# One-hot rows of a top-k expert layer stored as pairs of tokens instead of fours

## The chip, the cores and the metric

One core of a Trainium2 chip runs the kernel. The metric is the device time of one execution in microseconds. The kernel before takes 2242.8 us (median of 3 runs, 2241.6 to 2243.34).

## The reference

The reference is a small two-block network on 256 tokens of width 1024 (the second block adds 16 meta tokens). Each block ends in a layer of 16384 experts, of which every token chooses 8 heads x 16. What the change touches is the last part of this layer:

```python
idx  = top-k expert numbers of each token, 8 heads x 16      # expert = 128 * i + j
gate = softmax of their scores
act  = gelu(h . u_tab[idx])
out  = sum over the 128 choices of gate * act * v_tab[idx]
```

The kernel does not gather rows of u_tab and v_tab. It multiplies the tokens by all 16384 rows, takes gelu of everything, multiplies by a dense table of gates that is zero where an expert was not chosen, and multiplies the result by all of v_tab.

## The kernel before, in words

One expert layer (`peer`, run once for each block) has these stages. The queries and scores are computed; VectorE picks the top 16 of 16 lists (`choose`). Then `peer_act` runs a loop over 128 tiles of u: each tile is 24 matmuls (8 depth slices x 3, because every float32 factor is split in a high and a low part, L177 to L179) that give 128 experts x 256 tokens in PSUM; ScalarE takes gelu into the table `cb` (`evac`, L1107 and L1109). After that comes a loop over 128 tiles of v (`products`, L730).

The dense table of gates is built four tokens at a time by the generator `groups`, one group for each tile of u once `choose` is done, so 64 groups in each block. For a token t with 128 choices (on the partitions) it needs the sum over the choices of gate * onehot(i) x onehot(j). Three rows of numbers per token are ready in `lists`: i, j and the low part of the gate, all float16; the high part is rounded from `gates`. One group does the following.

- `hot(t0, 0)` (VectorE, L1002) compares `iota4` with i: for 4 tokens a 128 x 128 x 4 float16 tile `oi`, where the four tokens lie side by side behind each index, so an index is 8 bytes behind the one before.
- `weigh` makes `w`: four ScalarE activations (L1008), one for each token, multiply `oi` of that token by its gate; one VectorE multiply (L1009) by the low parts of the gates; then `hot(t0, 1)` (L1002) makes `oj`.
- `product` (TensorE, L1023) does 4 x 2 matmuls, each with its weight load: weights `oj` of one token, moving operand `w` (high, then low part), 128 columns, into a PSUM bank of 4 tokens x 128.
- `use` (VectorE, L1015) multiplies the part of `cb` that gelu has already filled by the PSUM tile; the rest is copied by ScalarE (L1036) and multiplied later, in `evac` (L1112).

The order of work is the order in which Python issues it; each engine runs its own stream in that order. `product` is put in a list, `middle`, and is issued by `tile_mm` between the 12th and 13th matmul of the next tile of u. Behind the 24 matmuls of a tile, ScalarE runs L1036, four times L1008, L1107, L1109 and the rounding of a later weight tile (L67); VectorE runs L1112, L1009, L1002 (`oj`), the subtraction for a weight tile (L70), L1015, L1002 (`oi`). Tiles of u come on SyncE's queue, 512 KB each, four buffers deep; their high and low parts are three deep. `choose` also reads the constant: its lookups (L970) take every fourth element of `iota4`.

Of the kernel before, what the change touches and what calls it, by code (L numbers as in the profile page):

```python
# [10 lines left out]
F16 = mybir.dt.float16  # L11
U32 = mybir.dt.uint32
AF = mybir.ActivationFunctionType
ALU = mybir.AluOpType
# [104 lines left out]
class Build:  # L119
# [743 lines left out]
    def peer_act(self, b, cpool, ps, cb, pair):  # L863

        nc, spawn = self.nc, self.spawn
# [9 lines left out]
        lists, gates = lg[:, :2 * T].bitcast(F16).rearrange("p (a t) -> p a t", a=4)[:, :3], lg[:, 2 * T:]  # L875
        iota = cb[:, 95, 0:128]
        nc.sync.dma_start(iota, self.A["iota"])
        nc.sync.dma_start(keys, self.A["keys" + b])
        iota4 = cpool.tile([128, 128, 4], F16, name="iota4")
        nc.vector.tensor_copy(iota4, iota[:, :, None].to_broadcast([128, 128, 4]))  # L880
        seen, rows, have = [0], [0], [0]
        def choose():

# [2 lines left out]
            def take(shape, dt=F32):  # L886
                n = int(np.prod(shape[1:]))
                t = scr[:, off[0]:off[0] + n]
                off[0] += n
                assert off[0] <= 8192  # L890
                if dt != F32:
                    t = t.bitcast(dt)
                if len(shape) == 2:
                    return t
                names = " ".join("abcd"[:len(shape) - 1])
                return t.rearrange("p (%s) -> p %s" % (names, names), **dict(zip("abcd", shape[1:])))
# [51 lines left out]
            for tt in range(2):  # L948
                off[0] = base
                ts, ti, bs, bp = top[tt]  # L950
                g0 = take([128, 128])
                g = g0.rearrange("p (a b) -> p a b", a=8)
                sm = take([128, 8])
                nc.vector.tensor_tensor(g, bs, bs[:, :, 0:1].to_broadcast([128, 8, 16]), op=ALU.subtract)
                nc.scalar.activation(g, g, AF.Exp)
                tf = take([128, 8, 2, 16])
                nc.vector.tensor_copy(tf, ti)
                ab = take([128, 2, 8, 16], U32)
                nc.vector.tensor_scalar(ab[:, 0], bp, 4, None, op0=ALU.logical_shift_right)
                nc.vector.tensor_scalar(ab[:, 1], bp, 15, None, op0=ALU.bitwise_and)  # L960
                af = take([128, 2, 8, 16])
                nc.vector.tensor_copy(af, ab)
                yield 1.0
                ij = take([128, 2, 8, 16])
                oh = take([128, 4, 16, 16])
                sh = [128, 4, 16, 16]
                for q in range(2):
                    for h0 in (0, 4):
                        hs = slice(h0, h0 + 4)
                        nc.vector.tensor_tensor(oh, iota4[:, None, None, 0:16, 0].to_broadcast(sh),  # L970
                                                af[:, q, hs, :, None].to_broadcast(sh), op=ALU.is_equal)
                        yield 1.1
                        nc.vector.tensor_tensor(oh, oh, tf[:, hs, q, None, :].to_broadcast(sh), op=ALU.mult)
                        yield 1.1
                        nc.vector.reduce_sum(ij[:, q, hs, :], oh, axis=AX.X)
                        yield 1.1
                nc.vector.reduce_sum(sm, g, axis=AX.X)
                nc.vector.reciprocal(sm, sm)
                nc.vector.tensor_tensor(g, g, sm[:, :, None].to_broadcast([128, 8, 16]), op=ALU.mult)
                yield 0.5  # L980
                p = ps.tile([128, 3, 128], F32, name="pl", tag="o")
                for q, src in enumerate((ij[:, 0], ij[:, 1], g)):
                    middle.append(lambda q=q, src=src: nc.tensor.transpose(
                        p[:, q, :], src.rearrange("p a b -> p (a b)"), self.ident))
                yield None
                ts = slice(tt * 128, tt * 128 + 128)
                nc.scalar.copy(lists[:, 0:2, ts], p[:, 0:2, :])
                nc.scalar.activation(gates[:, ts], p[:, 2, :], AF.Copy, scale=SCALE)

                hi = take([128, 64]).bitcast(F16)  # L990
                nc.scalar.activation(hi, p[:, 2, :], AF.Copy, scale=SCALE)
                nc.vector.tensor_sub(lists[:, 2, ts], gates[:, ts], hi)
                yield 0.5
        def groups():

            TG = 4

            sh = [128, 128, TG]

            def hot(t0, q):  # L1000
                o = cpool.tile(sh, F16, name="o" + "ij"[q], bufs=1 + q)
                nc.vector.tensor_tensor(o, iota4, lists[:, q, None, t0:t0 + TG].to_broadcast(sh), op=ALU.is_equal)  # L1002
                return o

            def weigh(t0, oi):
                w = cpool.tile([128, 2, 128, TG], F16, name="w", bufs=2)
                for j in range(TG):
                    nc.scalar.activation(w[:, 0, :, j], oi[:, :, j], AF.Copy, scale=gates[:, t0 + j:t0 + j + 1])  # L1008
                nc.vector.tensor_tensor(w[:, 1], oi, lists[:, 2, None, t0:t0 + TG].to_broadcast(sh), op=ALU.mult)  # L1009
                return hot(t0, 1), w  # L1010

            def use(t0, p):
                n = rows[0]
                c, pk = cb[:, :, t0:t0 + TG], p.rearrange("p t i -> p i t")
                nc.vector.tensor_tensor(c[:, :n, :], c[:, :n, :], pk[:, :n, :], op=ALU.mult)  # L1015
                copies = [(c[:, n:, :], pk[:, n:, :])] if n < 128 else []
                have[0] = t0 + TG
                return copies

            def product(p, oj, w):  # L1020
                for j in range(TG):
                    for q in range(2):
                        nc.tensor.matmul(p[:, j, :], oj[:, :, j], w[:, q, :, j], start=q == 0, stop=q == 1)  # L1023

            oi = hot(0, 0)
            yield
            w = weigh(0, oi)
            yield
            oi = hot(TG, 0)
            copies = []  # L1030
            for t0 in range(0, T, TG):
                p = ps.tile([128, TG, 128], F32, name="pg", **G[t0 // TG % 4])
                middle.append(lambda: product(p, *w))
                yield
                for c in copies:
                    nc.scalar.copy(*c)  # L1036
                nw = weigh(t0 + TG, oi) if t0 + TG < T else None
                yield
                copies = use(t0, p)
                if t0 + 2 * TG < T:  # L1040
                    oi = hot(t0 + 2 * TG, 0)
                w = nw
            for c in copies:
                nc.scalar.copy(*c)
            done[0] = True

        bg, credit, gg = choose(), [0.0], groups()
        busy, done = [True], [False]

# [28 lines left out]
        def tile_mm(kind):  # L1078
            wh, wl = (w.rearrange("p (k n) -> p k n", k=KC) for w in self.stream.get(kind))
            p = ps.tile([128, T], F32, name="pu", tag="mm", bufs=3)  # L1080
            for k in range(KC):
                if k == 4:
                    while middle:
                        middle.pop(0)()
                self.mm3(p, [((wh[:, k, :], wl[:, k, :]), (hh[:, k, :], hl[:, k, :]))], k == 0, k == KC - 1)
            self.step()
            return p
# [27 lines left out]
        for i in range(128):  # L1115
            p = tile_mm("u" + b)
# [613 lines left out]
```

## Time and profile before

| what | value |
| --- | --- |
| median of 3 runs | 2242.8 us |
| the profiled execution itself | 2251.93 us |
| its span, first to last instruction | 2250.1 us |
| TensorE matmul busy | 2210.9 us, 98% |
| TensorE weight load busy | 2024.1 us, 90% |
| VectorE busy | 1586.4 us, 71% |
| ScalarE busy | 1312.5 us, 58% |
| granted TensorE clock, mean | 0.998 of full speed |
| transfers, mean over the span | 172 GB/s |

Matmuls are pipelined, so the time of a stage is read from the distance between the starts of matmuls and not from the length of one record. Idle time of an engine that is not the bottleneck costs nothing. The groups run in two stretches of the span, 476 to 718 us and 1646 to 1889 us.

### The profile page before, as it was taken

What the parts mean: (1) busy time and instruction counts of PE and PEld (TensorE: products, weight loads), DVE (VectorE), ACT (ScalarE), POOL (GpSimd) and SP (SyncE); (2) the same over time, 40 slices, a digit from 0 to 9 for tenths busy, and PEclk for the clock granted to TensorE, in tenths of its full rate; (3) what the DMA queues carried; (4) which work ended last, traced back from release to release, by engine and by line L of the source; (5) the groups of instructions that cost most, each with busy time, mean ns of one, the idle gap of its engine ahead of it and who ended that gap; (6) DMA issues with size and microseconds to landing.
All of it is one profiled execution on the core that took longest, in us unless ns stands there. A gap on an engine that the chain in (4) does not pass through costs nothing.

```text
span 2250.1 us, 39324 instructions
## 1 busy us (share of the span) xinstructions
PE 2210.9 (98%) x15318; PEld 2024.1 (90%) x15318; DVE 1586.4 (71%) x3063; ACT 1312.5 (58%) x2480; POOL 0.2 (0%) x4
## 2 busy tenths in 40 slices
PE   6999999999999999999999999999999999999999
PEld 3998999999999888888888889999999999888887
DVE  5877699887777555665676556699877777555555
ACT  6565554567777444444675456544577776544443
POOL 0000000000000000000000000000000000000000
PEclk9999999999999999999999999999999999999999
DMA  7475556654444666776443336556654445666664
GB/s 263 157 241 184 199 178 188 177 171 141 141 141 142 196 192 194 214 228 208 152 130 94 91 106 181 162 177 188 178 161 141 141 140 160 188 192 193 195 192 154
DMA packets 108155, 386.49 MB, mean 172 GB/s; under 512 B 12784, under 2 KB 14128, under 8 KB 107712
## 3 DMA queue, kind: packets, MB, share of 16 engines
q1 hardware_dynamic: 107968, 383.98, 56.5%
q8 instruction: 120, 1.97, 0.4%
q14 instruction: 67, 0.55, 0.1%
HBM read 382.88 MB, written 1.05 MB: 171 GB/s over the span
## 4 chain that ended last, share of the span: by engine, by line
PE 93%; DVE 3%; ACT 3%; issue 1%; DMA 1%; SPq 0%; ACTq 0%; DVEq 0%
PE acc L730 31%; PE pu L179 12%; PE pu L177 12%; PE pu L178 11%; PE pg L1023 5%; PE pz L177 5%; PE pz L179 4%; PE pz L178 4%; DVE wlo L70 1%; ACT whi L67 1%; PE pa L1426 1%; PE sp L1070 1%; PE po L565 1%; PE S L1371 0%; DMA raw<-w_mod_a 0%
## 5 line engine op out<-in xcount | busy, mean ns | idle before, releaser
L70 DVE TENSOR_TENSOR wlo<-raw,whi 128x1024 fp32r<-128x1024 f32 x690 | 840.9, 1220 | 441.1 <-ACT whi L67 435.7
L67 ACT CAST whi<-raw 128x1024 fp32r<-128x1024 f32 x690 | 722.7, 1048 | 405.4 <-PE acc L730 349.0
L177 PE MATMUL pu<-hh,whi 128*128 128x256 f32 x2272 | 650.7, 286 | 0.0
L179 PE MATMUL pu<-hh,wlo 128*128 128x256 f32 x2272 | 637.2, 280 | 0.3
L178 PE MATMUL pu<-hl,whi 128*128 128x256 f32 x2272 | 637.0, 280 | 0.0
L179 PEld LDWEIGHTS pu<-hh,wlo 128*128 128x128 f32 x2272 | 430.4, 189 | 1.1 <-DVE wlo L70 1.1
L178 PEld LDWEIGHTS pu<-hl,whi 128*128 128x128 f32 x2272 | 431.2, 190 | 0.0
L177 PEld LDWEIGHTS pu<-hh,whi 128*128 128x128 f32 x2272 | 429.6, 189 | 0.0
L730 PE MATMUL acc<-whi,ch 128*128 128x512 f32 x1024 | 317.3, 390 | 0.0
L730 PE MATMUL acc<-wlo,ch 128*128 128x512 f32 x1024 | 316.6, 389 | 0.0
L730 PE MATMUL acc<-whi,cl 128*128 128x512 f32 x1024 | 316.5, 389 | 0.0
L730 PEld LDWEIGHTS acc<-whi,cl 128*128 128x128 f32 x1024 | 192.2, 188 | 40.0
L730 PEld LDWEIGHTS acc<-wlo,ch 128*128 128x128 f32 x1024 | 192.2, 188 | 39.9
L730 PEld LDWEIGHTS acc<-whi,ch 128*128 128x128 f32 x1024 | 191.6, 188 | 39.2
L1008 ACT ACTIVATE w<-oi,lists 128x128 f16<-128x128 f16 x512 | 192.8, 581 | 1.9 <-DVE oi L1002 1.4
L1109 ACT ACTIVATE cb<-pu 128x256 f32<-128x256 f32 (+32 forms) x250 | 82.2, 329 | 167.2 <-PE pu L179 166.9
L1015 DVE TENSOR_TENSOR cb<-cb,pg 128x248 f32<-128x248 f32 (+42 forms) x128 | 69.7, 544 | 114.9 <-ACT cb L1109 114.7
L1023 PE MATMUL pg<-w,oj 128*128 128x128 f16 x1024 | 142.2, 296 | 0.0
L1023 PEld LDWEIGHTS <-oj 128*128 128x128 f16 x1024 | 103.8, 118 | 6.8
L1107 ACT ACTIVATE gl<-pu 128x4 f32<-128x4 f32 (+21 forms) x132 | 37.3, 283 | 111.3 <-ACT w L1008 97.6
L706 DVE TENSOR_TENSOR cl<-cb,ch 128x256 fp32r<-128x256 f32 x256 | 96.4, 418 | 5.2 <-ACT ch L704 5.2
L177 PE MATMUL pz<-nh,whi 128*128 128x256 f32 (+1 forms) x328 | 97.0, 296 | 0.0
(420 smaller groups left out, 2928.7 us busy)
## 6 DMA issues: line engine op xcount, KB each, us to landing
raw<-u SPq DMA_DIRECT2D x256, 512.0 KB, 3.6
raw<-v SPq DMA_DIRECT2D x256, 512.0 KB, 3.7
raw<-w_mod_b SPq DMA_DIRECT2D x32, 512.0 KB, 4.3
raw<-pw_q SPq DMA_DIRECT2D x32, 512.0 KB, 3.8
raw<-w_in_z SPq DMA_DIRECT2D x28, 512.0 KB, 4.2
raw<-w_mod_a SPq DMA_DIRECT2D x16, 512.0 KB, 4.8
raw<-w_mix_out SPq DMA_DIRECT2D x8, 512.0 KB, 4.0
raw<-w_gv SPq DMA_DIRECT2D x8, 512.0 KB, 3.5
```

Of the source, the lines that this page charges most:

```text
L67: nc.scalar.copy(hi[:, :f], t[:, :f])
L70: nc.vector.tensor_sub(lo[:, :f], t[:, :f], hi[:, :f].bitcast(F32)), self.load_to(k + self.raw_bufs))
L177: self.nc.tensor.matmul(out, sh, mh, start=first and i == 0, stop=False)
L178: self.nc.tensor.matmul(out, sh, ml, start=False, stop=False)
L179: self.nc.tensor.matmul(out, sl, mh, start=False, stop=last and i == n - 1)
L706: nc.vector.tensor_sub(l[r], c[:, r, :], h[:, r, :].bitcast(F32))
L730: nc.tensor.matmul(acc[tt][dh], st[:, ts], mv[:, dh * 512:dh * 512 + 512], start=i == n == 0, stop=i == 127 and n == 2, skip_group_check=True)
L1008: nc.scalar.activation(w[:, 0, :, j], oi[:, :, j], AF.Copy, scale=gates[:, t0 + j:t0 + j + 1])
L1015: nc.vector.tensor_tensor(c[:, :n, :], c[:, :n, :], pk[:, :n, :], op=ALU.mult)
L1023: nc.tensor.matmul(p[:, j, :], oj[:, :, j], w[:, q, :, j], start=q == 0, stop=q == 1)
L1107: nc.scalar.activation(t[:, :n], p[:, :n], AF.Gelu)
L1109: nc.scalar.activation(row[:, n:], p[:, n:], AF.Gelu)
```

## The change

The four tokens of a group are stored as two pairs. A tile is now [pair 2][index 128][token of the pair 2] instead of [index 128][token 4], so an index of one token lies 4 bytes behind the index before instead of 8. The constant `iota4` (each index four times) becomes `iota2` (twice). The comparisons and the multiply go over a four-dimensional view, in which the numbers of two tokens repeat for 128 indices; the matmuls and the ScalarE activations address token j as pair j // 2, half j % 2. Counts of instructions, their elements and the order of work stay the same.

```diff
-        iota4 = cpool.tile([128, 128, 4], F16, name="iota4")
-        nc.vector.tensor_copy(iota4, iota[:, :, None].to_broadcast([128, 128, 4]))
+        iota2 = cpool.tile([128, 128, 2], F16, name="iota2")
+        nc.vector.tensor_copy(iota2, iota[:, :, None].to_broadcast([128, 128, 2]))
...
-                        nc.vector.tensor_tensor(oh, iota4[:, None, None, 0:16, 0].to_broadcast(sh),
+                        nc.vector.tensor_tensor(oh, iota2[:, None, None, 0:16, 0].to_broadcast(sh),
...
-            sh = [128, 128, TG]
+            sh = [128, TG // 2, 128, 2]
+
+            def of(q, t0):
+                l = lists[:, q, t0:t0 + TG].rearrange("p (g s) -> p g s", s=2)
+                return l[:, :, None, :].to_broadcast(sh)
...
-                nc.vector.tensor_tensor(o, iota4, lists[:, q, None, t0:t0 + TG].to_broadcast(sh), op=ALU.is_equal)
+                nc.vector.tensor_tensor(o, iota2[:, None].to_broadcast(sh), of(q, t0), op=ALU.is_equal)
...
-                w = cpool.tile([128, 2, 128, TG], F16, name="w", bufs=2)
+                w = cpool.tile([128, 2] + sh[1:], F16, name="w", bufs=2)
                 for j in range(TG):
-                    nc.scalar.activation(w[:, 0, :, j], oi[:, :, j], AF.Copy, scale=gates[:, t0 + j:t0 + j + 1])
-                nc.vector.tensor_tensor(w[:, 1], oi, lists[:, 2, None, t0:t0 + TG].to_broadcast(sh), op=ALU.mult)
+                    nc.scalar.activation(w[:, 0, j // 2, :, j % 2], oi[:, j // 2, :, j % 2], AF.Copy,
+                                         scale=gates[:, t0 + j:t0 + j + 1])
+                nc.vector.tensor_tensor(w[:, 1], oi, of(2, t0), op=ALU.mult)
...
-                        nc.tensor.matmul(p[:, j, :], oj[:, :, j], w[:, q, :, j], start=q == 0, stop=q == 1)
+                        nc.tensor.matmul(p[:, j, :], oj[:, j // 2, :, j % 2], w[:, q, j // 2, :, j % 2], start=q == 0,
+                                         stop=q == 1)
```

## Rows read from the trace of the kernel before

**Rows 1.** The page's busy times and its chain by line
```profile
PE 2210.9 (98%) x15318; PEld 2024.1 (90%) x15318; DVE 1586.4 (71%) x3063; ACT 1312.5 (58%) x2480; POOL 0.2 (0%) x4
...
PE acc L730 31%; PE pu L179 12%; PE pu L177 12%; PE pu L178 11%; PE pg L1023 5%; PE pz L177 5%; PE pz L179 4%; PE pz L178 4%; DVE wlo L70 1%; ACT whi L67 1%; PE pa L1426 1%; PE sp L1070 1%; PE po L565 1%; PE S L1371 0%; DMA raw<-w_mod_a 0%
```
**Rows 2.** Busy time by stretch: span; engines' busy us; granted clock; DMA share
```profile
476.00:718.00 242.00, 242.00 (x2052) 238.59 (x2052) 184.62 (x381) 189.90 (x512) 0.00 (x0) 1.00 0.48 140
...
1655.00:1890.00 235.00, 235.00 (x1992) 231.71 (x1990) 177.99 (x368) 183.47 (x494) 0.00 (x0) 1.00 0.47 141
```
**Rows 3.** The chain of waits in 476 to 718 us
```profile
by line: PE pg L1023 25.2%; PE pu L177 25.0%; PE pu L178 24.9%; PE pu L179 24.9%
...
495.78 0.95 PE pg L1023 x8
499.56 0.95 PE pg L1023 x8
```
**Rows 4.** TensorE around one product, in order of time: start, length, what
```profile
707.18 0.28 PE L179 MATMUL pu<-hh,wlo 128*128 128x256 f32 x1
707.31 1.11 PE L1023 MATMUL pg<-w,oj 128*128 128x128 f16 x8
...
708.37 0.28 PE L178 MATMUL pu<-hl,whi 128*128 128x256 f32 x1
...
709.78 0.28 PE L178 MATMUL pu<-hl,whi 128*128 128x256 f32 x1
```
**Rows 5.** Loop over v, matmuls of 512 columns in order of time
```profile
1000.41 0.62 PE L730 MATMUL acc<-whi,cl 128*128 128x512 f32 x2
1000.86 0.62 PE L730 MATMUL acc<-whi,ch 128*128 128x512 f32 x2
```
**Rows 6.** Matmuls and loads by line: busy us, mean ns, idle before
```profile
L1023 PE MATMUL pg<-w,oj 128*128 128x128 f16 x1024 | 142.2, 296 | 0.0
L1023 PEld LDWEIGHTS <-oj 128*128 128x128 f16 x1024 | 103.8, 118 | 6.8
```
**Rows 7.** Weight loads in order of time: f16, short float32; the latter by line
```profile
707.30 0.15 PEld L1023 LDWEIGHTS <-oj 128*128 128x128 f16 x2
...
29.13 0.56 PEld L375 LDWEIGHTS pmc<-ident,rows 4*128 4x128 f32 x8 [0.47 <-issue]
...
L375 PEld LDWEIGHTS pmc<-ident,rows 4*128 4x128 f32 x16 | 1.2, 136 | 2.5 <-ACT rows L369 2.0 <-issue 0.5
```
**Rows 8.** Plain float32 matmuls of 128 columns, in order of time
```profile
262.31 0.60 PE L1070 MATMUL sp<-cb 128*128 128x128 f32 x4
```
**Rows 9.** ScalarE through one group, in order of time, [idle before it]
```profile
703.86 1.49 ACT L1008 ACTIVATE w<-oi,lists 128x128 f16<-128x128 f16 x4
706.14 0.37 ACT L1107 ACTIVATE gl<-pu 128x240 f32<-128x240 f32 x1 [0.78 <-ACT w L1008]
```
**Rows 10.** ScalarE before the first group: two activations of 128 elements
```profile
474.42 0.28 ACT L988 ACTIVATE lists<-pl 128x128 f32<-128x128 f32 x1
...
474.58 0.28 ACT L991 ACTIVATE cb<-pl 128x128 f16<-128x128 f32 x1
```
**Rows 11.** Four instructions by line: lengths in ns, least/median/most
```profile
L1002 DVE TENSOR_TENSOR oj<-iota,lists x128: 412/418/423, 475.9 to 1882.4; 128x512 f16<-128x512 f16 x128
...
L1008 ACT ACTIVATE w<-oi,lists x512: 554/582/618, 475.6 to 1882.8; 128x128 f16<-128x128 f16 x171
...
L970 DVE TENSOR_TENSOR cb<-iota,cb x16: 1216/1218/1226, 410.1 to 1633.6; 128x1024 f32<-128x1024 f16 x16
...
L880 DVE CAST iota<-cb x2: 426/426/427, 257.4 to 1427.0; 128x512 f16<-128x512 f32 x2
```
**Rows 12.** Who waited for whom in 476 to 718: us, times, longest; one late product
```profile
DVE cb L1015 <- ACT cb L1109: 57.2, 63, 1.6
ACT gl L1107 <- ACT w L1008: 48.8, 61, 0.9
...
L1015 DVE TENSOR_TENSOR cb<-cb,pg 128x488 f32<-128x488 f32 x1 | 0.7, 665 | 0.7 <-ACT cb L1109 0.7
```

## The prediction

> **What bounds the kernel now.** I read the busy times and the chain first. TensorE is busy 98% of the span, and the chain that ended last lies almost wholly on it; the products of the gates (L1023) hold 5% of it [rows 1]. Next I asked for the two stretches in which groups are built: TensorE is busy 242.0 of 242.0 us and 235.0 of 235.0, at full granted clock, while VectorE and ScalarE are each busy about three quarters of the time [rows 2]. So what TensorE saves there is saved for good, until another engine becomes as long. The chain in the first stretch gives L1023 a quarter of the time, 0.95 us for each run of eight matmuls, and a group comes every 3.78 us (495.78 to 499.56) [rows 3].
>
> Then I went to one product in order of time. From the last matmul of the first half tile (707.18) to the second matmul of the second half (708.37) pass 1.19 us; twelve ordinary steps take 1.41 (708.37 to 709.78), 0.118 each. Taking off two such steps, the eight pairs of load and matmul cost 0.954 us, which agrees with the 0.95 of the chain: 0.119 us for each pair [rows 3, 4].
>
> This is odd, and the change rests on it. A matmul of 128 float16 columns costs as much as one of 256 split-float32 columns. What does a column cost? In the loop over v two matmuls of 512 columns take 0.452 us (1000.41 to 1000.86), 0.226 each [rows 5]. From 256 to 512 columns the step grows from 0.118 to 0.226, so 256 columns cost 0.109, 128 cost 0.0545, and about 0.009 is fixed for each pair [rows 4, 5]. At that rate 128 columns should take 0.0635. The pair takes 0.118: its columns come at half the rate. The record of one matmul says the same: 296 ns, longer than the 280 of 256 columns [rows 4, 6].
>
> Is the load what takes long instead? Its record has 118 ns, the same as the pair's distance, which is suspicious [rows 6]. But the first two loads of a run together end 0.15 us after the first began, and each lasts about 0.12, so the second began within some 0.03 of the first: a load can be taken in quickly [rows 7]. And eight short loads at L375 take 0.56 us together with 0.136 for each, so they start 0.06 apart, though each record is twice as long as that: a record's length is latency and not what a pair must wait [rows 7]. So I put the 0.118 down to the moving operand, whose columns lie 8 bytes apart in `w`, where the split-float32 ones lie 4 bytes apart and come at full rate.
>
> **The change part by part.** *The matmuls (L1023).* Number and columns stay; the step of both operands falls from 8 to 4 bytes, which is the step of the float32 operands that run at one column per step of the fast rate. I take the full rate: 0.118 becomes 0.0635, so 8 x 0.0545 = 0.436 us per group. Nothing else is on the path (TensorE has no idle time there), and there are 2 x 64 groups: 128 x 0.436 = 55.8 us. Bounds: without the fixed 0.009 a group would save 0.51 us, 65 us in all; if the columns keep their rate, nothing. A loss I leave out here: no row has a 4-byte step slower than this pair. Plain float32 at L1070 has a 4-byte step and comes every 0.11 us ((0.60 - 0.28) / 3) for 128 columns, also the half rate, but that is another kind of number [rows 8]; it counts for the third rival.
>
> [...]
>
> *Other waits in the group.* The period falls from 3.78 to 3.34 us. ScalarE idles 0.78 us per group before L1107 (waiting for the tile, though the row names its own last instruction), so 0.34 is left [rows 9, 12]. VectorE idles before L1015 57.2 / 63 = 0.91 us on average and about 0.7 late in the stage, when L1015 is longest; 0.26 is left there [rows 12]. Tiles of u come at 140 GB/s [rows 2], which becomes about 158, less than the 172 of the whole span. Nothing becomes late, but little is left.
>
> *VectorE's comparisons and multiply (L1002 twice, L1009).* Elements stay at 512. Now a run of two numbers repeats instead of four. I cost it at zero: L970 reads a number repeated in every element and still takes one element per step (1024 in 1218 ns), so a repeated word is no obstacle [rows 11]. Bounds: zero, or the rate of float32 products, 665 ns for 488 elements (so about 690 for 512) against 418, +0.27 each and +0.8 us per group [rows 11, 12]. I take zero, since the innermost run is still dense and even; above 0.26 per group it begins to show.
>
> *ScalarE's four activations (L1008).* They read and write every second number instead of every fourth. Four take 1.49 us with records of 0.58: one starts every 0.30 [rows 9, 11]. Dense ones start 0.16 apart (474.42 to 474.58) [rows 10]. Bounds: 0.16 (worth nothing, as ScalarE is off the path) to 0.58, one wholly after the other. I take 0.30 or less; ScalarE's idle time covers it up to 0.39.
>
> *The constant.* L880 copies 256 instead of 512 elements, twice: less than 0.43 us each, behind TensorE's query matmuls; zero. L970 reads every second instead of every fourth number at one element per step; zero [rows 11].
>
> **The sum.** The profiled execution took 2251.9 us, 1.8 more than its span of 2250.1. Minus 55.8 it is 2196.1. The median of the runs is 0.9960 of that execution, so 2187.
>
> **The rivals.**
> 1. *Full rate, as above:* 2187, chance 0.59. Its own range, with 50 to 65 us saved, is 2178 to 2193.
> 2. *The load becomes the bound.* The first f16 load of a run starts 0.12 after the matmul ahead of it, where a float32 load starts beside it [rows 4, 7]; perhaps it does not overlap with columns. Then the pair stops between 0.0635 and 0.118. Halfway, 0.09, it saves 8 x 0.028 x 128 = 29 us: 2214. Chance 0.15.
>  [...]
> 3. *The rate does not depend on 8 or 4 bytes* (any step of float16 halves it, or the load's 118 ns is what each pair waits for). Then 2243, no change. For it: each matmul begins as its load's record ends. Against it: rows 7. Chance 0.13.
> 4. *VectorE falls to the float32 rate.* Its work per group is 3.78 - 0.91 = 2.87 and becomes 3.67, longer than 3.34. VectorE then sets the pace and 0.11 x 128 = 14 us are saved: 2229. Chance 0.06.
> 5. *Slower: ScalarE's activations run one after the other.* Tokens of a pair now write the two halves of the same words over a denser range. Place: L1008; its work per group is 3.78 - 0.78 = 3.00 us, and four full records of 0.58 (2.33 instead of 1.49) make 3.84. That is over the present period by 0.06: 128 x 0.06 = +8 us, 2251. It eats into the gain from a spacing of 0.39 on and turns it to a loss from 0.50 on. Against it: tokens 0 and 1 share words already, at 0.30. Chance 0.07.
>
> **How the numbers follow.** The likeliest case gives 2187. The range 2178 to 2232 holds cases 1, 2 and 4, about 0.80; cases 3 and 5 are left out. This kernel's measurement tells about 0.2% (4.5 us) from no change. Faster by more: 0.59 + 0.15 + 0.06 = 0.80; within it 0.13; slower 0.07.
>
> **What would show it.** Right: L1023's matmul record falls from 296 to about 240 ns, its run of eight in the chain from 0.95 to about 0.52 us, a group comes every 3.34 us, TensorE stays without idle time in these stretches, L1002 and L1009 stay at 418 ns, and the idle time before L1107 falls to about 0.34 and before L1015 to about 0.5 on average. Wrong: a product that still takes 0.95 (case 3) or about 0.75 (case 2); 690 ns at L1002 with idle TensorE (case 4); L1008 starting 0.5 us apart (case 5). A gain of the other stages would mean that I missed something: all of it should lie in the two stretches.

## The result, and the profile after

The kernel after takes 2193.98 us (median of 4 runs, 2188.84 to 2196.8), against 2242.74 for the kernel before in the same comparison: a ratio of 0.9771, with a 95% interval of 0.9757 to 0.9785. A second comparison gave 2190.38 against 2245.29, 0.9757 [0.9743, 0.9771]. So 49 to 55 us went. The forecast was 2187, with 2178 to 2232 as its range. The profiled execution of the kernel after took 2196.02 us with a span of 2194.0, 56.1 less than the span before.

The busy times and the chain by line come first, as in [rows 1]:

```profile
PE 2156.2 (98%) x15318; PEld 1970.3 (90%) x15318; DVE 1585.6 (72%) x3063; ACT 1289.5 (59%) x2480; POOL 0.2 (0%) x4
...
PE acc L730 32%; PE pu L177 12%; PE pu L179 12%; PE pu L178 12%; PE pz L177 5%; PE pz L179 4%; PE pz L178 4%; PE pg L1029 3%; DVE wlo L70 1%; ACT whi L67 1%; PE pa L1433 1%; PE sp L1077 1%; PE po L565 1%; PE S L1378 1%; PE pu L224 1%
```

The numbers of instructions are the same as before on every engine, and TensorE is still busy 98%. It is busy for 55 us less (2210.9 before), and the share of the products on the chain falls from 5% to 3%. L1023 is L1029 now; L1002, L1009 and L1008 are L1007, L1015 and L1013; L1107, L1109 and L1015 are L1114, L1116 and L1021.

Then the two stretches in which groups are built, with the columns of [rows 2]:

```profile
476.00:690.00 214.00, 214.00 (x2045) 211.20 (x2043) 184.68 (x383) 178.78 (x510) 0.00 (x0) 1.00 0.53 157
...
1628.00:1835.00 207.00, 207.00 (x1973) 204.32 (x1973) 177.04 (x367) 170.42 (x488) 0.00 (x0) 1.00 0.54 158
```

These windows are chosen to hold nearly the same matmuls (2045 for 2052, 1973 for 1992), and they are 214 and 207 us long instead of 242 and 235. From the start of the first product to the start of the last pass 211.9 us in either block, where it was 238.8 and 239.0: 54.0 us less in all. TensorE still has no idle time in them, at full granted clock, and the DMA rate has risen from 140 to 157 GB/s. The chain in the first stretch, as in [rows 3]:

```profile
by line: PE pu L177 29.6%; PE pu L179 28.1%; PE pu L178 28.0%; PE pg L1029 14.3%
...
481.53 0.48 PE pg L1029 x8
488.25 0.48 PE pg L1029 x8
```

Between these two lies one more group: 6.72 us for two, 3.36 each, where a group took 3.78. One product in order of time (start, length, what), as in [rows 4]:

```profile
602.09 0.28 PE L179 MATMUL pu<-hh,wlo 128*128 128x256 f32 x1
602.22 0.64 PE L1029 MATMUL pg<-w,oj 128*128 128x128 f16 x8
602.66 0.36 PE L177 MATMUL pu<-hh,whi 128*128 128x256 f32 x1
602.86 0.28 PE L178 MATMUL pu<-hl,whi 128*128 128x256 f32 x1
```

From the last matmul before the run to the second one behind it pass 0.77 us. Less two ordinary steps of 0.118 that is 0.53 for the product, where the same sum gave 0.954 before [rows 4]. So a product saves 0.42, and 128 of them 54 us of the 56. The other 2 us lie outside the group stretches, where ordinary steps differ from one execution to the next (last section). Note that the step from L177 to L178 is 0.20 and not 0.118. It was so before, too, from this line to 708.37 [rows 4]:

```profile
708.17 0.36 PE L177 MATMUL pu<-hh,whi 128*128 128x256 f32 x1
```

So this step alone is no new cost, and only the sum up to L178 can be compared: from the start of the last float16 matmul to L178 pass 0.227 us now and 0.249 before (medians of the 128 products). Each pair became 0.06 shorter, this stretch only 0.022: the return to float32 costs something here that it did not cost before. The chain counts this at L177, which is why its share is larger than that of L178.

The matmul and the load of the product by line, as in [rows 6], and three instructions by line, as in [rows 11]:

```profile
L1029 PE MATMUL pg<-w,oj 128*128 128x128 f16 x1024 | 81.2, 220 | 0.0
L1029 PEld LDWEIGHTS <-oj 128*128 128x128 f16 x1024 | 58.9, 97 | 5.6
```

```profile
L1013 ACT ACTIVATE w<-oi,lists x512: 420/443/469, 476.8 to 1827.5; 128x128 f16<-128x128 f16 x171
...
L1007 DVE TENSOR_TENSOR oj<-iota,lists x128: 415/419/423, 477.2 to 1827.1; 128x512 f16<-128x512 f16 x128
...
L970 DVE TENSOR_TENSOR cb<-iota,cb x16: 1217/1218/1227, 410.9 to 1604.1; 128x1024 f32<-128x1024 f16 x16
```

The matmul's record fell from 296 to 220 ns, the load's from 118 to 97, ScalarE's activation from 582 to 443. VectorE's comparison stayed (418 before, 419 now), and so did L970. At last the waits, as in [rows 12] (total us, times, longest):

```profile
ACT gl L1114 <- ACT w L1013: 33.7, 61, 0.6
DVE cb L1021 <- ACT cb L1116: 30.2, 63, 1.2
```

ScalarE idles 33.7 / 61 = 0.55 us per group before L1114, VectorE 30.2 / 63 = 0.48 before L1021. Both have come nearer to setting the pace, and neither does.

### The profile page after: what moved, and what is told of

Its sections match the earlier page's. It is cut to its first block, busy times and chain, and to the rows that moved or that the text cites. A ratio compares the mean times of both kernels' runs of the same rounds, so it can differ in the third digit from the quotient of the medians.

```text
span 2194.0 us, 39324 instructions
## 1 busy us (share of the span) xinstructions
PE 2156.2 (98%) x15318; PEld 1970.3 (90%) x15318; DVE 1585.6 (72%) x3063; ACT 1289.5 (59%) x2480; POOL 0.2 (0%) x4
## 4 chain that ended last, share of the span: by engine, by line
PE 92%; DVE 3%; ACT 3%; DMA 1%; issue 1%; SPq 0%; ACTq 0%; DVEq 0%
PE acc L730 32%; PE pu L177 12%; PE pu L179 12%; PE pu L178 12%; PE pz L177 5%; PE pz L179 4%; PE pz L178 4%; PE pg L1029 3%; DVE wlo L70 1%; ACT whi L67 1%; PE pa L1433 1%; PE sp L1077 1%; PE po L565 1%; PE S L1378 1%; PE pu L224 1%
## 5 line engine op out<-in xcount | busy, mean ns | idle before, releaser
L177 PE MATMUL pu<-hh,whi 128*128 128x256 f32 x2272 | 649.3, 286 | 0.0
L178 PE MATMUL pu<-hl,whi 128*128 128x256 f32 x2272 | 635.6, 280 | 0.0
L178 PEld LDWEIGHTS pu<-hl,whi 128*128 128x128 f32 x2272 | 431.2, 190 | 0.0
L177 PEld LDWEIGHTS pu<-hh,whi 128*128 128x128 f32 x2272 | 426.7, 188 | 0.0
L1116 ACT ACTIVATE cb<-pu 128x256 f32<-128x256 f32 (+32 forms) x250 | 81.9, 328 | 163.6 <-PE pu L179 163.4
L1013 ACT ACTIVATE w<-oi,lists 128x128 f16<-128x128 f16 x512 | 170.3, 442 | 1.9 <-DVE oi L1007 1.4
L1021 DVE TENSOR_TENSOR cb<-cb,pg 128x248 f32<-128x248 f32 (+42 forms) x128 | 69.7, 544 | 60.7 <-ACT cb L1116 60.7
L177 PE MATMUL pz<-nh,whi 128*128 128x256 f32 (+1 forms) x328 | 97.0, 296 | 0.0
L179 PE MATMUL pz<-nh,wlo 128*128 128x256 f32 (+1 forms) x328 | 93.2, 284 | 0.0
L178 PE MATMUL pz<-nl,whi 128*128 128x256 f32 (+1 forms) x328 | 92.9, 283 | 0.0
L1114 ACT ACTIVATE gl<-pu 128x4 f32<-128x4 f32 (+21 forms) x132 | 37.3, 283 | 79.6 <-ACT w L1013 67.3
```

The source lines that it names most:

```text
L177: self.nc.tensor.matmul(out, sh, mh, start=first and i == 0, stop=False)
L178: self.nc.tensor.matmul(out, sh, ml, start=False, stop=False)
L179: self.nc.tensor.matmul(out, sl, mh, start=False, stop=last and i == n - 1)
L1013: nc.scalar.activation(w[:, 0, j // 2, :, j % 2], oi[:, j // 2, :, j % 2], AF.Copy, scale=gates[:, t0 + j:t0 + j + 1])
L1114: nc.scalar.activation(t[:, :n], p[:, :n], AF.Gelu)
L1116: nc.scalar.activation(row[:, n:], p[:, n:], AF.Gelu)
```

## The experiments

The theory after the result: a matmul's columns come at a rate set by the step of its moving operand `w`, and the weights' step hardly matters. The rivals: the load is what became faster (its record fell too, 118 to 97); or 8 bytes are as good as 4, as the forecast's third rival had it, and something else is at work. After that, the size: the run costs 0.53 where 8 x 0.0635 = 0.51 had been forecast. Is that the pair's own cost, or something that each run pays once?

**Only the moving operand at 4 bytes.** `oi` and `w` as in the kernel after; `oj`, the weights, in fours as before (`four` repeats the numbers of four tokens for 128 indices).

```diff
+        iota4 = cpool.tile([128, 128, 4], F16, name="iota4")
+        nc.vector.tensor_copy(iota4, iota[:, :, None].to_broadcast([128, 128, 4]))
...
+                if q == 1:
+                    o = cpool.tile([128, 128, TG], F16, name="o" + "ij"[q], bufs=1 + q)
+                    nc.vector.tensor_tensor(o, iota4, four(q, t0), op=ALU.is_equal)
+                    return o
...
-                        nc.tensor.matmul(p[:, j, :], oj[:, j // 2, :, j % 2], w[:, q, j // 2, :, j % 2], start=q == 0,
+                        nc.tensor.matmul(p[:, j, :], oj[:, :, j], w[:, q, j // 2, :, j % 2], start=q == 0,
```

> Only the moving operand w (and oi, from which it is made) is laid out in pairs, 4 bytes from one index to the next; the weights oj stay in fours, 8 bytes. Theory A (the step of the moving operand sets the rate of the columns): the matmul of L1023 is as in the changed kernel, record about 220 ns, pairs about 58 ns apart, a product about 0.53 us, a group every 3.36 us, time 2194 (2188 to 2200). Rival B (the weight load with its 8-byte step is what each pair waits for): as before, record 296, pairs 118 apart, a group every 3.78, time 2243. ScalarE's activations: about 440 ns under both, since w and oi have the new layout.

Measured: 2191.23 us, 0.9758 [0.9742, 0.9774]; the same as the kernel after. Its matmul and load (ns: least/median/most), and a product in order of time:

```profile
L1038 PEld LDWEIGHTS <-oj x1024: 111/113/136, 471.4 to 1828.0; 128*128 128x128 f16 x171
...
L1038 PE MATMUL pg<-w,oj x1024: 217/221/252, 471.4 to 1828.1; 128*128 128x128 f16 x171
```

```profile
602.14 0.28 PE L179 MATMUL pu<-hh,wlo 128*128 128x256 f32 x1
602.26 0.67 PE L1038 MATMUL pg<-w,oj 128*128 128x128 f16 x8
602.73 0.36 PE L177 MATMUL pu<-hh,whi 128*128 128x256 f32 x1
602.93 0.28 PE L178 MATMUL pu<-hl,whi 128*128 128x256 f32 x1
```

The product takes 0.79 - 0.236 = 0.55 us (0.558 as the median of all 128; the kernel after has 0.530). So the weights' step of 8 bytes costs 28 ns per product, and its record stays long (113) while the pairs follow each other in 59. All of the gain but these 28 of 424 ns is the moving operand's.

**Only the weights at 4 bytes.** The reverse: `oj` in pairs, `oi` and `w` in fours.

```diff
-                w = cpool.tile([128, 2] + sh[1:], F16, name="w", bufs=2)
+                w = cpool.tile([128, 2, 128, TG], F16, name="w", bufs=2)
...
-                        nc.tensor.matmul(p[:, j, :], oj[:, j // 2, :, j % 2], w[:, q, j // 2, :, j % 2], start=q == 0,
+                        nc.tensor.matmul(p[:, j, :], oj[:, j // 2, :, j % 2], w[:, q, :, j], start=q == 0,
```

> The other half alone: the weights oj in pairs (4 bytes), w and oi in fours (8 bytes). Theory A: no change of time, 2243 (2238 to 2248), pairs 118 ns apart, a group every 3.78 us, though the load's record may fall from 118 to about 97 ns. Rival B: all of the gain, 2194, pairs about 58 apart. If both halves are needed, this one and the moving half alone both stay at 2243.

Measured: 2241.77 us, 0.9991 [0.9977, 1.0004]: no change.

```profile
L1037 PEld LDWEIGHTS <-oj x1024: 96/116/119, 469.6 to 1874.0; 128*128 128x128 f16 x171
L1037 PE MATMUL pg<-w,oj x1024: 276/296/300, 469.6 to 1874.1; 128*128 128x128 f16 x171
```

The matmul's record is the old 296 ns, and a product costs 0.937 us as the median of all, 16 ns less than before. The load's record did not fall to 97 either but stayed at 116, while in the run just told it was 113 with pairs 59 apart: its length does not tell how long a pair takes. The load is not what the old pair waited for.

**The moving operand at 16 bytes.** `w` holds high and low part of four tokens side by side, so its columns lie 16 bytes apart; the weights stay in pairs.

```diff
-                w = cpool.tile([128, 2] + sh[1:], F16, name="w", bufs=2)
+                w = cpool.tile([128, 128, 2, TG], F16, name="w", bufs=2)
...
-                        nc.tensor.matmul(p[:, j, :], oj[:, j // 2, :, j % 2], w[:, q, j // 2, :, j % 2], start=q == 0,
+                        nc.tensor.matmul(p[:, j, :], oj[:, j // 2, :, j % 2], w[:, :, q, j], start=q == 0,
```

> High and low part of w are interleaved, so the moving operand's step becomes 16 bytes; weights in pairs (4 bytes), oi in fours. Theory A1 (a column costs one step of the fast rate for each 4 bytes of the operand's step): four steps a column, 213 ns for 128 columns, pairs 215 to 230 apart, record near 400 ns, a group every 4.6 to 4.7 us, time about 2243 + 1024 x 0.105 = 2350 (2335 to 2365). Rival A2 (any step above 4 bytes simply halves the rate): pairs 118 apart, 2243. [...]

Measured: 2354.08 us, 1.0489 [1.0471, 1.0506]. A product in order of time, the first stretch by engine, and ScalarE's activation:

```profile
600.35 0.28 PE L179 MATMUL pu<-hh,wlo 128*128 128x256 f32 x1
600.47 1.99 PE L1037 MATMUL pg<-w,oj 128*128 128x128 f16 x8
602.10 0.48 PE L177 MATMUL pu<-hh,whi 128*128 128x256 f32 x1
602.41 0.28 PE L178 MATMUL pu<-hl,whi 128*128 128x256 f32 x1
```

```profile
480.00:760.00 280.00, 280.00 (x1923) 230.07 (x1922) 177.44 (x362) 247.18 (x484) 0.00 (x0) 1.00 0.39 115
```

```profile
L1022 ACT ACTIVATE w<-oi,lists x512: 866/1096/1132, 468.6 to 1982.7; 128x128 f16<-128x128 f16 x171
```

The product takes 2.06 - 0.236 = 1.82 us (1.83 as the median): 0.229 for each pair. TensorE has no idle time, so this is its own pace and not a wait, although ScalarE's activation took 1096 ns. The rate went on falling in proportion to the step: 0.0575 at 4 bytes, 0.118 at 8, 0.229 at 16. A flat half rate for every float16 step that isn't dense is out with that. As an estimate from the loop over v [rows 4, 5], a column at the fast rate costs (0.226 - 0.118) / 256 us, or 0.42 ns; four of these for each of 128 columns make 0.216 us, where the expectation had 213 ns and the run shows 0.229.

**Dense.** Every one-hot row by itself, 2 bytes from one index to the next. That leaves one number of `lists` repeated 128 times in VectorE's innermost dimension.

```diff
-            sh = [128, TG // 2, 128, 2]
+            sh = [128, TG, 128]
...
-                l = lists[:, q, t0:t0 + TG].rearrange("p (g s) -> p g s", s=2)
-                return l[:, :, None, :].to_broadcast(sh)
+                return lists[:, q, t0:t0 + TG, None].to_broadcast(sh)
...
-                        nc.tensor.matmul(p[:, j, :], oj[:, j // 2, :, j % 2], w[:, q, j // 2, :, j % 2], start=q == 0,
+                        nc.tensor.matmul(p[:, j, :], oj[:, j], w[:, q, j], start=q == 0,
```

> All four tokens one behind the other, 2 bytes from one index to the next, for oi, oj and w. Theory A: the columns are at full rate already at 4 bytes, so pairs stay 57 to 58 ns apart and a product at 0.53 us. VectorE now repeats one number for 128 indices. If that costs its two-a-step rate (690 instead of 419 ns at each of three instructions, +0.8 us per group) VectorE sets the pace with 2.9 + 0.8 = 3.7 us per group, TensorE gets idle time, and the time is about 2194 + 128 x 0.33 = 2236 (2215 to 2245). If it does not, 2194 (2188 to 2200).

Measured: 2218.11 us, 0.9876 [0.986, 0.9893].

```profile
L1028 PE MATMUL pg<-w,oj x1024: 218/219/231, 477.5 to 1856.2; 128*128 128x128 f16 x171
...
L1006 DVE TENSOR_TENSOR oj<-iota,lists x128: 682/705/761, 476.8 to 1855.0; 128x512 f16<-128x512 f16 x128
```

```profile
480.00:700.00 220.00, 210.23 (x1970) 198.94 (x1968) 219.97 (x367) 173.07 (x492) 0.00 (x0) 1.00 0.50 149
```

```profile
PEld L1028 <- DVE oj L1006: 20.4, 55, 0.6
```

Two things are told apart here. The matmul gains almost nothing below 4 bytes: its record is 219 ns against 220, and pairs come every 0.056 (the median from start to start) instead of 0.0575. And VectorE's comparison takes 705 ns instead of 419, so VectorE is busy 219.97 of 220.00 us and TensorE waits for `oj`. This is the forecast's fourth rival, in a kernel that isn't the one forecast: what decides here is whether the innermost dimension holds two numbers (419 ns) or one (705). (The multiply, L1014 there, took 706.)

**Each product as two runs of four pairs.** The first two tokens behind the float32 matmuls of one step of the tile, the others behind a later step.

```diff
-            def product(p, oj, w):
-                for j in range(TG):
+            def product(p, oj, w, j0):
+                for j in range(j0, j0 + 2):
...
-                middle.append(lambda: product(p, *w))
+                middle.extend([lambda: product(p, *w, 0), lambda: product(p, *w, 2)])
...
-                if k == 4:
-                    while middle:
+                if k in (3, 5):
+                    half = len(middle) // 2 if k == 3 and len(middle) == 2 else 0
+                    while len(middle) > half:
```

> The changed kernel with each product issued as two runs of four pairs, behind the 9th and the 15th matmul of a tile instead of eight pairs behind the 12th. In the changed kernel a product costs 530 ns, of which 8 x 57.5 = 460 are the pairs. Theory C: the other 70 ns are paid once for each run, when the engine goes from float32 to float16 and back (the float32 load behind the run needs longer than one short matmul covers). Two runs then cost 600 ns, a group comes every 3.43 us, and the time is 128 x 0.07 = 9 us above the changed kernel, about 2202. Rival D: the 70 ns belong to the pairs (66 each); then nothing changes, 2193.

Measured: 2197.19 us, 0.9804 [0.9781, 0.9826]; the kernel after, on the same chip, 2190.38. The profiled span is 2195.0 against 2187.3. One run of four in order of time:

```profile
601.25 0.28 PE L179 MATMUL pu<-hh,wlo 128*128 128x256 f32 x1
601.38 0.41 PE L1029 MATMUL pg<-w,oj 128*128 128x128 f16 x4
601.59 0.36 PE L177 MATMUL pu<-hh,whi 128*128 128x256 f32 x1
601.79 0.28 PE L178 MATMUL pu<-hl,whi 128*128 128x256 f32 x1
```

It costs 0.54 - 0.236 = 0.30 us (0.299 as the median), not half of 0.53. Two of them make 0.60, 0.07 more than one run of eight; 128 x 0.07 = 9 us. The two loops over tiles of u show 9.2 (441.8 and 441.9 us against 437.1 and 437.5); the spans show 7.7, since other stages happened to be shorter.

**The products of two groups in one run of sixteen.** Every second tile carries both; `w` and `oj` have three buffers, and a group's result is used one group later.

```diff
-                o = cpool.tile(sh, F16, name="o" + "ij"[q], bufs=1 + q)
+                o = cpool.tile(sh, F16, name="o" + "ij"[q], bufs=1 + 2 * q)
...
-                middle.append(lambda: product(p, *w))
+                both.append((p, w))
+                if len(both) == 2:
+                    middle.append(lambda two=tuple(both): [product(a, *b) for a, b in two])
+                    both.clear()
...
-                copies = use(t0, p)
+                copies = use(t0 - TG, last) if t0 else []
+                last = p
```

> The changed kernel with the products of two groups issued as one run of sixteen pairs in every second tile (three buffers instead of two for w and oj; the multiplication by cb comes one group later). Theory C: one change of number format less for two groups, 70 ns saved for every second group: 64 x 0.07 = 4.5 us, about 0.2%, so 2189 where the changed kernel has 2193.5. Rival D: no change. If the later multiplication or the uneven load (one tile of 2.83 us, the next of 3.8) makes VectorE or ScalarE late, it is slower instead: each has 3.0 us of work per tile, more than 2.83.

Measured: 2182.65 us, 0.9734 [0.971, 0.9759]; the span is 2182.4 against 2187.3. One run:

```profile
633.58 0.28 PE L179 MATMUL pu<-hh,wlo 128*128 128x256 f32 x1
633.70 1.09 PE L1029 MATMUL pg<-w,oj 128*128 128x128 f16 x16
634.60 0.36 PE L177 MATMUL pu<-hh,whi 128*128 128x256 f32 x1
634.80 0.28 PE L178 MATMUL pu<-hl,whi 128*128 128x256 f32 x1
```

It costs 1.22 - 0.236 = 0.98 us (0.989 as the median). So runs of 4, 8 and 16 pairs cost 0.299, 0.530 and 0.989. The differences give (0.530 - 0.299) / 4 = 0.0577 and (0.989 - 0.530) / 8 = 0.0574 for a pair, and 0.530 - 8 x 0.0575 = 0.07 that each run pays once. With 64 such costs saved, 64 x 0.07 = 4.5 us were to be won, and the spans show 4.9 (the loops over tiles of u 5.5). The third buffer also reaches tiles of the loop over v; that loop takes 353.0 us in the first block in both kernels, so it has no part in the gain. This version is the fastest of all by its median, 7.7 us below the kernel after; the two ratios' intervals overlap (0.971 to 0.9759 and 0.9743 to 0.9771), so the gain over the kernel after is likely and not settled by times alone. The product's cost in the trace is.

**The kernel after again, and the kernel before profiled again.** Both without an edit, beside the two kernels just told.

> The changed kernel once more, on the same chip as the two variants of it, for their comparison: 2193 (2188 to 2197), a product 530 ns, a group every 3.36 us.

> The kernel before, profiled a second time. Its profiled execution took 2251.9 us where its other runs have a median of 2242.8. If that execution was only long by chance, this one shows 2240 to 2246 with the product still at 0.95 us, and the difference lies in the distance of ordinary matmuls (118 or 113.5 ns); if profiling makes it longer, 2251 to 2253 again.

Measured: 2190.38 us for the kernel after, with a profiled span of 2187.3 and again 0.53 per product. The profiled execution of the kernel before took 2245.48 (span 2243.4), with 0.953 per product as in the first profile, but 6.7 us less in span than that. The difference lies in the float32 tiles ahead of the groups: from the first matmul of u to the first product pass 220.2 and 220.3 us in the two blocks of the first profile, and 215.3 in both of the second (other stages were 3 us longer there). L177 by line in 340 to 400 us (busy us, mean ns), first of the first profile of before, then of the second:

```profile
L177 PE MATMUL pu<-hh,whi 128*128 128x256 f32 x171 | 48.1, 281 | 0.0
```

```profile
L177 PE MATMUL pu<-hh,whi 128*128 128x256 f32 x178 | 49.1, 276 | 0.0
```

In the same 60 us stand 171 matmuls of this line in one execution and 178 in the other: with three such lines, a step of 60 / (3 x 171) = 0.117 us against 0.112 (0.118 and 0.113 from start to start). TensorE has no idle time in either, and the kernel is the same. What sets the level isn't known.

## Why the prediction was right, point by point

- **The moving operand's step: right, and shown.** The step "0.118 becomes 0.0635" rested on the columns at half rate because they lie 8 bytes apart. The first two experiments put all but 28 of the 424 ns per product on `w`, the third shows the rate falling on in proportion to the step, to 0.229 us for a pair at 16 bytes.
- **Its size: two errors that nearly cancel.** The pair was taken at 0.0635, with a fixed 0.009 from float32 matmuls; it measured 0.0575, so 8 x 0.006 = 0.05 us per group more was won. But a run of fast pairs pays about 0.07 for going from float32 to float16 and back, which the forecast did not have; before it was 0.01, since 0.953 - 8 x 0.118 leaves no more. So 0.06 per group was lost. Together 0.436 + 0.05 - 0.06 is about 0.42 per group: 54 us instead of 55.8. That the cost comes once per run is shown by the runs of 4 and 16. Most of it lies behind the run, where 0.0575 + 0.118 = 0.176 would do and 0.227 pass up to L178; before, 0.249 passed where 0.236 would do. Why it is there is only argued. The loads of the kernel after show that the first float32 load behind the run starts 0.03 us ahead of its matmul (602.63 and 602.66), where an ordinary one starts 0.11 ahead (601.98 and 602.09), and that the next load comes 0.11 later (602.74):

```profile
601.98 0.19 PEld L179 LDWEIGHTS pu<-hh,wlo 128*128 128x128 f32 x1
602.21 0.46 PEld L1029 LDWEIGHTS <-oj 128*128 128x128 f16 x8
602.63 0.19 PEld L177 LDWEIGHTS pu<-hh,whi 128*128 128x128 f32 x1
602.74 0.19 PEld L178 LDWEIGHTS pu<-hl,whi 128*128 128x128 f32 x1
```

  A last pair of 0.118 would cover such a load and one of 0.0575 would not. But the kernel before has nearly as short a lead there (its load starts at 708.12, its matmul at 708.17) at almost no cost, so the lead by itself does not show the cost; no run separates this from another cost of the change of kind.
- **The profiled execution: 2196.1 forecast, 2196.0 measured. The step from it to the median failed.** The forecast scaled by 0.9960, the ratio of before's median to its profile, and came to 2187; the medians are 2194 and 2190. The second profile of before shows why. The float32 tiles ahead of the groups took 220.2 and 220.3 us in the first and 215.3 twice in the second, so the first profile was some 7 us long by chance; in the profile of after they took 220.6 and 215.8, so it was long too, in one block. That 2196.1 was met to 0.1 us is luck: the groups gave 54.0 us and these tiles 4.1, while the other stages took 2.0 longer. One profile cannot tell such a surplus from a constant ratio, and an offset that belongs to one execution should not have been carried to the other kernel.
- **VectorE at 418: right in the number, wrong in one reason.** L1007 takes 419 and L1015 420. What the forecast calls a step is 1.045 ns, as an estimate from two sizes of the float32 product in the kernel before (L1015 there), (675 - 420) / (500 - 256), with 0.152 us on top for each instruction:

```profile
L1015 DVE TENSOR_TENSOR cb<-cb,pg 128x500 f32<-128x500 f32 x1 | 0.7, 675 | 1.6 <-ACT cb L1109 1.6
...
L1015 DVE TENSOR_TENSOR cb<-cb,pg 128x256 f32<-128x256 f32 x1 | 0.4, 420 | 1.1 <-ACT cb L1109 1.1
```

  By that, 1024 elements at one per step take 1.22 us, which is the 1218 ns of L970, and 512 at two per step 0.42. "A repeated word is no obstacle" was concluded from L970, which runs at one element per step anyway and so could not show what costs the faster rate. The other reason held, the innermost run "still dense and even": with one number repeated, in the dense version, it is 705 against 419, close to the bound of 690 that the forecast gave.
- **ScalarE: right.** Four activations took 1.33 us with records of 0.443, so they start (1.33 - 0.443) / 3 = 0.30 apart, as before; the fifth rival needed 0.39. The row:

```profile
602.46 1.33 ACT L1013 ACTIVATE w<-oi,lists 128x128 f16<-128x128 f16 x4
```

  The idle time before L1114 is 0.55 rather than 0.34, since the four take 1.33 instead of 1.49 and the forecast gave that no value. VectorE's 0.48 before L1021 meets the forecast 0.5.
- **The second rival (the load becomes the bound)** is out: the pairs came at 0.0575, and with the slow load of 113 ns still at 0.059.
- **The third rival (8 or 4 bytes are alike)** is out: a pair took 0.0575 at 4 bytes and 0.118 at 8.
- **The matmul's record** was forecast at 240 and is 220; its run in the chain 0.52 and 0.48; a group 3.34 and 3.36. The run of eight was read as 0.95 in the chain before and as 0.954 by start-to-start; after, the chain's 0.48 misses the cost of the return, which it counts at L177.

## What to carry to other kernels

Where TensorE bounds, compare what a column costs in each of its matmuls: if one kind costs twice as much (here 118 ns for 128 float16 columns, as for 256 split-float32 ones), look at the byte step of its moving operand before anything else. For float16, 4 bytes from column to column were enough here: 57.5 ns a pair, against 118 at 8 bytes and 56 at 2. The weights' step mattered far less: 8 bytes instead of 4 cost 28 of the 424 ns per product. Two tokens side by side serve both engines: the matmul is within 1.5 ns of the dense pair, and VectorE's repeated operand still has two different numbers next to each other (419 ns), where the dense layout loses on VectorE (705 ns) more than it could win: 2218 us against 2194. Put short float16 runs together among float32 work (4, 8 and 16 pairs cost 0.299, 0.530 and 0.989 us), and take a second profile of the kernel before when a few us of its own time enter the sum.

## What the runs showed of the hardware that was not expected

- A matmul of 128 float16 columns took 56, 57.5, 118 and 229 ns per pair at steps of 2, 4, 8 and 16 bytes of the moving operand: from 4 bytes on in proportion to the step.
- Going from float32 to float16 matmuls and back cost about 70 ns per run when the float16 pairs were fast, and about 10 when each took 118.
- ScalarE's activation of 128 float16 elements had records of 387, 443 and 582 ns at steps of 2, 4 and 8 bytes (1096 when it read at 8 and wrote at 16), yet up to 8 bytes they started 0.29 to 0.31 apart all the same.
- The same float32 matmuls, without any wait, stepped in 0.113 or in 0.118 us, by execution and by stretch of the program. One and the same stretch took about 215 or 220 us by it; its cause is open.
